# Two pairs of plain tiles instead of four in the second and third feed-forward blocks of a decoder trunk, with ten seven-product blocks instead of nine

## The chip, the cores and the metric

One NeuronCore of a Trainium2 chip. The metric is the device time of one execution of the whole kernel in microseconds, the median over the runs shown.

## The reference

Two layers run on x of 512 x 1024 in float32. Each layer is

```
h += 1/2 SwiGLU(RMSNorm(h));  h += Mixer(RMSNorm(h));  h += 1/2 SwiGLU(RMSNorm(h))
def swiglu(x, w_in, w_out):
    gate, up = jnp.split(x @ w_in, 2, axis=-1)      # w_in 1024 x 5632, w_out 2816 x 1024
    return (jax.nn.silu(gate) * up) @ w_out
```

The first layer's mixer is sparse attention with top-k keys, the second's a gated MLP over chunks of 128 positions; a last RMSNorm follows. So there are four feed-forward blocks: the first before the attention, the second and third directly one after the other, the fourth at the end.

## The kernel before, in words

**Data.** The stream `h` lies transposed in SBUF, as 8 tiles of 128 features by 512 positions. Each matrix product is done in three passes (`mul3`, L345): weights and activations are split into a high and a low part (fp32r), and high x high, high x low and low x high are added up in PSUM. XH[k], XL[k] are the two parts of the input times the norm's gain. The norm's own factor is multiplied in afterwards, at the gates and at the output.

**Weights.** `WeightStream` loads all weights in one order, PLAN (L47 to L51). A letter "P" is one load of 8 tiles of 128 x 128 and one unit; a letter "S" is one block of the seven-product form: four loads (r11, r21, r22, r12) and seven units F0 to F6. A unit is converted before use: ScalarE writes the high part (L184), VectorE the low part (L187). `_prepare` (L140) does the additions that some of the F units need, on VectorE: two sums at L158 for F1 and F2, L161 for F4, L163 for F5. They are issued one unit ahead, between the high and the low part of the unit before. The converted units lie in a ring `w` of three, and F units also in a ring `x` of two; at a unit "P" the converter goes up to four units ahead as far as the rings allow (`_next`, L196), and after each product of a form block up to five (`ahead`, L207).

**A feed-forward block** (`ffn`, L415) has 22 gate tiles and 22 up tiles of 128 features, in 22 pairs. Its input product runs plainly for the first four pairs and in the seven-product form for the other 18:

- A *group* (L355) computes two pairs in four PSUM banks, eight steps k of 12 matmuls with 512 columns (128 weights x 512 positions). Its weights are units P0 to P3, two k each. Hooks after the steps place the norm and the sums: after k = 3 the split of the squares (`parts_of_squares`), after k = 5 the column sums on TensorE (L384), VectorE's wait for them (`vcol`, L387) and the reciprocal root, after k = 7 the factor spread over rows (L394 on TensorE, then the copies `rb`, `rh` on ScalarE).
- `sums(kp)` (L448) builds for each pair of k tiles the four sums that the form needs, TH[kp] and TL[kp]: two scaled copies on ScalarE (L453), four differences on VectorE (L455 to L458), then two splits, each a copy `th` on ScalarE and a difference `tl` on VectorE (L370, L371). sums(0), (1), (2) are issued after k = 5, 6, 7 and sums(3) behind `plain_gates`, the multiplication of the gates by the norm (L497).
- `rest` (L590 to L616): four single products, for pairs 2 and 3, 24 matmuls of 512 columns each.
- Then blocks of the form. `two_pairs` (L508) computes two pairs in seven products of 24 matmuls with 256 columns, in three banks A, B, C. `right(f, kp)` says what a product reads: products 0, 3 and 5 read XH, XL, products 1, 2, 4 and 6 read TH, TL, for the four kp one after the other:

```
product(0, A, True, True, "m1")     # XH, XL; then ScalarE copies A
product(1, C, True, True, "m5")     # TH[kp][:, 0], TL[kp][:, 0], kp = 0..3
product(2, A, False, True, "u2")    # adds into A
```

The form blocks come in three chunks (2, 4 and 3 of them); after each chunk the output product adds its part to `h`. The first block has hooks of its own and another order; the fourth ends with the last norm.

**Order.** The order on each engine is that of the program (a manual schedule); VectorE, ScalarE and SyncE's queue of loads run theirs one after the other. `step` and `later` put the gates' further work (up, as_y) behind the products.

Of the kernel before, what the change touches and what calls it, by code (L numbers as in the profile page):

```python
# [19 lines left out]
P = 128  # L20
D = 1024
S = 512
KD = D // P
# [20 lines left out]
HALF = S // 2  # L44


PLAIN = 4  # L47
CHUNKS = (2, 4, 3)
FFN_PLAN = "P" * 8 + "SS" + "P" * 8 + "SSSS" + "P" * 8 + "SSS" + "P" * 6
PLAN = FFN_PLAN + "P" * 37 + FFN_PLAN + FFN_PLAN + "P" * 72 + FFN_PLAN  # L50
LAST = 2 * CHUNKS[-1]  # L51
WARM = 24
N_LOADS = sum(4 if k == "S" else 1 for k in PLAN)
N_PIECES = N_LOADS * LOAD
# [3 lines left out]
class WeightStream:  # L58
# [8 lines left out]
    def __init__(self, nc, pool, dram):  # L67
# [3 lines left out]
        self.loads, self.units = [], []  # L71
        for kind in PLAN:
            base, n = len(self.units), len(self.loads)
# [93 lines left out]
    def _convert_to(self, n):  # L167
        while self.converted < min(n, len(self.units)):
            u = self.converted
            kind, i, f = self.units[u]  # L170
            kept = u >= len(self.units) - LAST
            rings = [r for r in ("w", "x")[:1 if kind == "P" and not kept else 2]
                     if self._free(r, len(self.units) - LAST if kept else self.current)
                     and self._free(r, self.current)]
# [67 lines left out]
def tile_trunk(ctx: ExitStack, tc, specs_out, xT, wst, gT, gl, rel, onehot, bu, bv, lng, lnb, wspT, bsp, out):  # L242
# [10 lines left out]
    def uname(s):  # L253
        counter[0] += 1
        return f"{s}_{counter[0]}"
# [8 lines left out]
    def bank(tag="acc"):  # L264
        return psum.tile([P, 512], F32, tag=tag, bufs=4, name=uname(tag))
# [38 lines left out]
    acc = [None]  # L304
# [40 lines left out]
    def mul3(ps, w, x, first, last, **kw):  # L345

        (wh, wl), (xh, xl) = w, x
        mm(ps, wh, xh, start=first, stop=False, **kw)  # L348
        mm(ps, wh, xl, start=False, stop=False, **kw)  # L349
        mm(ps, wl, xh, start=False, stop=last, **kw)  # L350
# [14 lines left out]
    def single(ps, c, K, spec, parts=x_parts):  # L365
        for k in range(K):
            mul3(ps, W.take(spec(k, c)), parts(k), k == 0, k == K - 1)
# [5 lines left out]
    def parts_of_squares():  # L373

        ah = small.tile([P, S], F32R, tag="s0_512", bufs=1, name=uname("ah"))
        al = small.tile([P, S], F32R, tag="s1_512", bufs=1, name=uname("al"))
        split(acc[0], ah, al)
        return ah, al
# [33 lines left out]

        return {k: parts, k + 1: columns, k + 2: rows}

    def ffn(layer, which, norm, finish, begin=None, hooks=None, aside=None, last=None, tags=("acc", "aux")):  # L415

# [3 lines left out]

        NJ = DFF // P
        KP = KD // 2
        tag_of = lambda i: tags[i % 2]
        n1, n2 = slice(0, HALF), slice(HALF, S)
        with tc.tile_pool(name=uname("ffn"), bufs=1) as fp:
            W.spool = fp
# [4 lines left out]
            def gate_tile():  # L433
                return fp.tile([P, 2, S], F32, tag="gate", bufs=2, name=uname("gate"))
# [13 lines left out]
            def sums(kp):  # L448

                xg, t = [temp("m1"), temp("m5")], [temp("u2"), temp("u3")]  # L450
                for i in range(2):
                    k = 2 * kp + i
                    nc.scalar.activation(xg[i], H[k], AF.Copy, scale=g_sb[:, norm, k:k + 1])  # L453
                tt = nc.vector.tensor_tensor
                tt(t[0][:, n1], xg[0][:, n2], xg[0][:, n1], op=ALU.subtract)  # L455
                tt(t[0][:, n2], xg[1][:, n2], xg[0][:, n2], op=ALU.subtract)
                tt(t[1][:, n1], xg[1][:, n2], t[0][:, n1], op=ALU.subtract)
                tt(t[1][:, n2], xg[1][:, n1], t[1][:, n1], op=ALU.subtract)  # L458
                for i in range(2):
                    split(t[i], *(x[kp][:, 2 * i:2 * i + 2].rearrange("p a b -> p (a b)") for x in (TH, TL)))  # L460
# [15 lines left out]
            R, Y, later = {}, [], []  # L476
# [10 lines left out]
            def step():  # L487
                for _ in range(min(1, len(later))):
                    later.pop(0)()
# [5 lines left out]
            def plain_gates(banks, g):  # L495
                for i in range(2):
                    nc.vector.tensor_tensor(g[:, i], banks[2 * i], R["b"], op=ALU.mult)  # L497

            def plain_pairs(banks, g):
                nc.scalar.activation(g, g, AF.Silu)  # L500

                def up():
                    for i in range(2):
                        nc.vector.tensor_tensor(g[:, i], g[:, i], banks[2 * i + 1], op=ALU.mult)
                later.append(up)
                later.append(lambda: as_y(g))
# [59 lines left out]
            def scale():  # L566
                R["ps"] = R.get("ps") or bank(tags[1])
                R["c"] = scale_columns(R["ps"], R["sq"])

            def spread():  # L570
                R["b"], R["h"] = scale_rows(R["c"], R["ps"])
# [13 lines left out]

            banks = [bank(tags[0]) for _ in range(4)]
            group(banks, [0, NJ, 1, NJ + 1], KD, spec_in, hooks={k: lambda k=k: hook(k) for k in range(KD)})
            g = [gate_tile() for _ in range(2)]
            R["ps"] = R.get("ps") or bank(tags[1])
            rest = [bank(tags[1]) for _ in range(2)]  # L590
            if not hooks:
                plain_gates(banks, g[0])
            single(rest[0], 2, KD, spec_in)
            if hooks:
                R["sq"] = parts_of_squares()
                scale()
            else:
                plain_pairs(banks, g[0])
                sums(3)
            single(rest[1], NJ + 2, KD, spec_in)  # L600
            if hooks:
                spread()
                plain_gates(banks, g[0])
            step()
            rest.append(bank(tags[1]))
            single(rest[2], 3, KD, spec_in)
            step()
            if hooks:
                plain_pairs(banks, g[0])
            plain_gates(rest, g[1])  # L610
            rest.append(bank(tags[1]))
            single(rest[3], NJ + 3, KD, spec_in)
            step()
            if hooks:
                step()
            plain_pairs(rest, g[1])  # L616
            done, n_dp = 0, 0
            for ci, dps in enumerate(CHUNKS):
                p0 = done
                if ci:  # L620
                    Y.clear()
                done += 2 * dps
                if ci == 0:
                    done += PLAIN
                for i in range(dps):
                    pair = PLAIN + 2 * n_dp
                    between = ()
                    if aside:
                        aside(n_dp)
                    if last and n_dp == sum(CHUNKS) - 1:  # L630
                        between = last[0](bank("acc"), gate_tile)
                    two_pairs(pair, tag_of(n_dp), between)
                    n_dp += 1
                flush()
                n_k = done - p0
                tag0 = tag_of(n_dp)
                tag1 = tag_of(n_dp + 1)

                def spec_out(k, c, p0=p0):
                    return ("ffn_w_out", (layer, which), (p0 + k) * P, [(0, c * P, P)])  # L640

                def y_parts(k, s=slice(0, S)):
                    return Y[k // 2][0][:, k % 2, s], Y[k // 2][1][:, k % 2, s]

                end = ci == len(CHUNKS) - 1
                if end and last:
                    W.extra = [x[0].rearrange("p a b -> p (a b)") for x in (TH, TL)]
                    last[1](n_k, spec_out, y_parts, R["c"], temp)
                    continue
                if end:  # L650
                    W.spool = None

                def add(j, ps):
                    t = gate_tile()[:, 0]
                    nc.vector.tensor_tensor(t, ps, R["h"], op=ALU.mult)
                    nc.vector.tensor_tensor(H[j], H[j], t, op=ALU.add)
                    if end:
                        finish(j)

                first = [bank(tag0) for _ in range(4)]  # L660
                group(first, range(4), n_k, spec_out, y_parts)
                for j in range(4):
                    add(j, first[j])
                for j in range(4, KD):
                    ps = bank(tag1)
                    single(ps, j, n_k, spec_out, y_parts)
                    add(j, ps)
# [415 lines left out]
    def into(norm):  # L1083
        return lambda j: prepare(j, norm)
# [10 lines left out]
    with tc.tile_pool(name="bias", bufs=1) as bp:  # L1095
        table, dist = [], []

        def begin(spare):
# [4 lines left out]
        ffn(0, 0, 0, into(1), begin, {k: lambda k=k: behind(k) for k in range(KD)},  # L1103
            aside=lambda i: 0 < i <= HEADS and spread_bias(*dist, i - 1))
    mixer_a(dist[1], 2)
    ffn(0, 1, 2, into(3))
    ffn(1, 0, 3, into(4), tags=("aux", "acc"))
    mixer_b(5)


# [137 lines left out]
```

## Time and profile before

| | |
|---|---|
| median of 3 runs | 2093.56 us (2093.43 to 2094.03) |
| the profiled execution | 2093.53 us, of it a span of 2091.7 us |
| granted TensorE clock, mean | 0.998 of full speed |
| VectorE, ScalarE, GpSimd busy | 71%, 43%, 4% of the span |
| matmuls | 12252 |
| read from HBM | 205.67 MB, 101 GB/s over the span |
| second, third feed-forward block: first matmul | 621.8, 968.3 us |

The times of the rows further down count from the start of the span. Each operation has a line of the program; where a helper issues it, the name of what it writes tells the place. TensorE's matmuls are pipelined, so the distance between two starts, not the duration of one, is what one costs.

### The profile page before, as it was taken

What the parts mean: (1) busy time and instruction counts of PE and PEld (TensorE: products, weight loads), DVE (VectorE), ACT (ScalarE), POOL (GpSimd) and SP (SyncE); (2) the same over time, 40 slices, a digit from 0 to 9 for tenths busy, and PEclk for the clock granted to TensorE, in tenths of its full rate; (3) what the DMA queues carried; (4) which work ended last, traced back from release to release, by engine and by line L of the source; (5) the groups of instructions that cost most, each with busy time, mean ns of one, the idle gap of its engine ahead of it and who ended that gap; (6) DMA issues with size and microseconds to landing.
All of it is one profiled execution on the core that took longest, in us unless ns stands there. A gap on an engine that the chain in (4) does not pass through costs nothing.

```text
span 2091.7 us, 29771 instructions
## 1 busy us (share of the span) xinstructions
PE 2076.6 (99%) x12252; PEld 1844.4 (88%) x12252; DVE 1476.7 (71%) x2046; ACT 894.3 (43%) x1157; POOL 78.1 (4%) x57
## 2 busy tenths in 40 slices
PE   8999999999999999999999999999999999999998
PEld 7989898888888999898989999888888888989897
DVE  7768686597767678677968677645846466778676
ACT  6535344434446345354625344432323245535253
POOL 0000000143200000000000000000000000000000
PEclk9999999999999999999999999999999999999999
DMA  4233332222123222222333222422222222323321
GB/s 174 98 117 109 112 110 92 100 96 90 68 72 110 101 101 101 101 101 82 111 106 107 101 102 81 152 91 91 91 101 83 89 91 91 111 94 109 110 93 71
DMA packets 59001, 209.72 MB, mean 100 GB/s; under 512 B 6824, under 2 KB 6872, under 8 KB 58736
## 3 DMA queue, kind: packets, MB, share of 16 engines
q1 hardware_dynamic: 55584, 198.73, 27.4%
q0 software_dynamic: 1408, 5.38, 0.8%
q10 hardware_dynamic: 1872, 3.70, 0.5%
q8 instruction: 96, 1.57, 0.3%
q14 instruction: 41, 0.34, 0.1%
HBM read 205.67 MB, written 4.74 MB: 101 GB/s over the span
## 4 chain that ended last, share of the span: by engine, by line
PE 97%; DVE 2%; ACT 1%; issue 0%; ACTq 0%; DVEq 0%
PE acc L348 16%; PE acc L349 16%; PE acc L350 16%; PE aux L348 12%; PE aux L350 12%; PE aux L349 12%; PE acc L990 1%; PE aux L992 1%; PE aux L990 1%; PE acc L992 1%; PE acc L991 1%; PE aux L991 1%; PE aux L1040 1%; PE acc L908 1%; PE aux L872 1%; PE aux L896 0%
## 5 line engine op out<-in xcount | busy, mean ns | idle before, releaser
L187 DVE TENSOR_TENSOR wlo<-raw,whi 128x1024 fp32r<-128x1024 f32 (+1 forms) x382 | 463.4, 1218 | 296.7 <-ACT whi L184 296.3
L184 ACT ACTIVATE whi<-raw 128x1024 fp32r<-128x1024 f32 (+1 forms) x409 | 426.2, 1050 | 470.4 <-PE acc L349 192.0
L348 PE MATMUL acc<-xh,whi 128*128 128x512 f32 (+1 forms) x864 | 299.2, 346 | 1.7 <-ACT xh L309 1.6
L349 PE MATMUL acc<-xl,whi 128*128 128x512 f32 (+1 forms) x864 | 289.5, 335 | 1.1 <-DVE xl L310 1.1
L350 PE MATMUL acc<-xh,wlo 128*128 128x512 f32 (+1 forms) x864 | 289.1, 335 | 0.0
L348 PE MATMUL aux<-xh,whi 128*128 128x256 f32 (+1 forms) x616 | 196.9, 320 | 0.0
L350 PE MATMUL aux<-xh,wlo 128*128 128x256 f32 (+1 forms) x616 | 196.5, 319 | 0.0
L349 PE MATMUL aux<-xl,whi 128*128 128x256 f32 (+1 forms) x616 | 196.4, 319 | 0.0
L348 PEld LDWEIGHTS acc<-xh,whi 128*128 128x128 f32 x864 | 164.8, 191 | 20.0 <-ACT xh L309 2.6
L349 PEld LDWEIGHTS acc<-xl,whi 128*128 128x128 f32 x864 | 165.0, 191 | 18.7 <-DVE xl L310 2.0
L350 PEld LDWEIGHTS acc<-xh,wlo 128*128 128x128 f32 x864 | 164.8, 191 | 16.9
L348 PE MATMUL acc<-th,whi 128*128 128x256 f32 x608 | 172.4, 284 | 0.0
L350 PE MATMUL acc<-th,wlo 128*128 128x256 f32 x608 | 172.1, 283 | 0.0
L349 PE MATMUL acc<-tl,whi 128*128 128x256 f32 x608 | 172.0, 283 | 0.0
L348 PE MATMUL aux<-th,whi 128*128 128x256 f32 x544 | 154.0, 283 | 0.0
L349 PE MATMUL aux<-tl,whi 128*128 128x256 f32 x544 | 154.0, 283 | 0.0
L350 PE MATMUL aux<-th,wlo 128*128 128x256 f32 x544 | 154.0, 283 | 0.0
L348 PE MATMUL acc<-yh,whi 128*128 128x512 f32 x328 | 127.7, 389 | 0.0
L349 PE MATMUL acc<-yl,whi 128*128 128x512 f32 x328 | 127.7, 389 | 0.0
L348 PE MATMUL aux<-yh,whi 128*128 128x512 f32 x328 | 127.6, 389 | 0.0
L349 PE MATMUL aux<-yl,whi 128*128 128x512 f32 x328 | 127.6, 389 | 0.0
L350 PE MATMUL acc<-yh,wlo 128*128 128x512 f32 x328 | 127.6, 389 | 0.0
(292 smaller groups left out, 4404.9 us busy)
## 6 DMA issues: line engine op xcount, KB each, us to landing
raw<-in_wst SPq DMA_DIRECT2D x372, 512.0 KB, 3.2
dist<-dist_rows ACTq DMA_DIRECT2D x8, 320.0 KB, 4.2
h<-in_xT SPq DMA_DIRECT2D x8, 256.0 KB, 6.4
tb<-dist POOLq DMA_DIRECT2D x8, 256.0 KB, 3.9
bias<-in_bv POOLq DMA_DIRECT2D x1, 1536.0 KB, 7.5
raw<-in_wst SPq DMA_DIRECT2D x2, 256.0 KB, 3.5
wT<-in_wspT POOLq DMA_DIRECT2D x1, 512.0 KB, 9.3
bs<-in_bsp POOLq DMA_DIRECT2D x1, 512.0 KB, 11.4
```

The source lines that it names most:

```text
L184: self.nc.scalar.activation(hi[:, s], src[:, s], AF.Copy)
L187: self.lo_engine.tensor_tensor(lo[:, s], src[:, s], hi[:, s].bitcast(F32), op=ALU.subtract)
L348: mm(ps, wh, xh, start=first, stop=False, **kw)
L349: mm(ps, wh, xl, start=False, stop=False, **kw)
L350: mm(ps, wl, xh, start=False, stop=last, **kw)
L872: mm(ps[:, :n], QK[h, 0][:, b * P:(b + 1) * P], QK[h, 1][:, :n], start=True, stop=True)
L908: mm(po[0][:, b * P:(b + 1) * P], V[j][:, h * P:(h + 1) * P], pT[:, j * P:(j + 1) * P], start=j == 0, stop=j == b)
L990: mm(banks[t], xh, wh, start=k == 0, stop=False)
L991: mm(banks[t], xl, wh, start=False, stop=False)
L992: mm(banks[t], xh, wl, start=False, stop=k == KD - 1)
L1040: mm(ps[:, t * P:(t + 1) * P], V[t][:, d * P:(d + 1) * P], wT[:, g, :], start=True, stop=True)
```

## The change

The second and third feed-forward blocks are called with `plain=2`: only the group's two pairs run plainly, `rest` is left out, and 20 pairs run in the form, in chunks of 3, 4 and 3 blocks. `plain_gates`, `sums(3)` and `plain_pairs` then follow the group directly, and the first form block stands behind them. PLAN has, for these two blocks, four "P" fewer at the head and one "S" more. `tag_of` is shifted by one there, so that the first form block takes the banks that `rest` had. The other two blocks keep `plain=4` with the same order as before.

```diff
-PLAIN = 4
-CHUNKS = (2, 4, 3)
-FFN_PLAN = "P" * 8 + "SS" + "P" * 8 + "SSSS" + "P" * 8 + "SSS" + "P" * 6
-PLAN = FFN_PLAN + "P" * 37 + FFN_PLAN + FFN_PLAN + "P" * 72 + FFN_PLAN
+BLOCKS = {4: (2, 4, 3), 2: (3, 4, 3)}
+def ffn_plan(plain):
+    chunks = BLOCKS[plain]
+    return "P" * 2 * plain + "".join("S" * n + "P" * (2 * n + plain * (i == 0)) for i, n in enumerate(chunks))
+PLAN = ffn_plan(4) + "P" * 37 + ffn_plan(2) + ffn_plan(2) + "P" * 72 + ffn_plan(4)
...
-        tag_of = lambda i: tags[i % 2]
+        chunks = BLOCKS[plain]
+        tag_of = lambda i: tags[(i + (plain == 2)) % 2]
...
             group(banks, [0, NJ, 1, NJ + 1], KD, spec_in, hooks={k: lambda k=k: hook(k) for k in range(KD)})
-            g = [gate_tile() for _ in range(2)]
+            g = [gate_tile() for _ in range(plain // 2)]
             R["ps"] = R.get("ps") or bank(tags[1])
...
+            if plain == 2:
+                plain_gates(banks, g[0])
+                sums(3)
+                plain_pairs(banks, g[0])
+            else:
+                rest = [bank(tags[1]) for _ in range(2)]
...
-                    pair = PLAIN + 2 * n_dp
+                    pair = plain + 2 * n_dp
...
-    ffn(0, 1, 2, into(3))
-    ffn(1, 0, 3, into(4), tags=("aux", "acc"))
+    ffn(0, 1, 2, into(3), plain=2)
+    ffn(1, 0, 3, into(4), plain=2, tags=("aux", "acc"))
```

## Rows read from the trace of the kernel before

**Rows 1.** The profile's page: the busy time of each engine (part 1, with its share of the span and its instructions in brackets), and the weight loads of part 6 (count, KB each, median us from issue to landing).

```profile
PE 2076.6 (99%) x12252; PEld 1844.4 (88%) x12252; DVE 1476.7 (71%) x2046; ACT 894.3 (43%) x1157; POOL 78.1 (4%) x57
...
raw<-in_wst SPq DMA_DIRECT2D x372, 512.0 KB, 3.2
```

**Rows 2.** The waits of TensorE over the whole span: which instruction waited for which, us in total, times, longest us. The two rows that lie in the first feed-forward block.

```profile
PE acc L348 <- ACT xh L309: 1.6, 1, 1.6
PE acc L349 <- DVE xl L310: 1.1, 2, 0.8
```

**Rows 3.** Stretches of the third feed-forward block: from and to (us from the span's start), length, then busy us and instructions of TensorE, its weight loads, VectorE, ScalarE and GpSimd, the granted TensorE clock, the DMA share and GB/s. First the four single products of `rest`, then the first and the second block of the seven-product form.

```profile
991.83:1013.71 21.88, 21.88 (x99) 18.12 (x98) 19.35 (x30) 14.64 (x20) 0.00 (x0) 1.00 0.27 97
1013.71:1033.87 20.16, 20.16 (x170) 20.15 (x169) 19.75 (x22) 12.35 (x15) 0.00 (x0) 1.00 0.30 105
1033.87:1054.03 20.16, 20.16 (x171) 20.16 (x170) 14.36 (x16) 9.36 (x11) 0.00 (x0) 1.00 0.31 105
```

**Rows 4.** VectorE in order of time in the third feed-forward block, from the end of the norm's preparation to the first form block: start us, us, engine, line, operation, output and inputs, count, and in brackets the idle time before it and what ended it.

```profile
977.00 2.36 DVE L187 TENSOR_TENSOR wlo<-raw,whi 128x1024 fp32r<-128x1024 f32 x2
979.27 0.69 DVE L371 TENSOR_TENSOR al<-sqacc,ah 128x512 fp32r<-128x512 f32 x1
...
985.64 0.16 DVE L387 TENSOR_SCALAR vcol<-acc 128x4 f32<-128x4 f32 x1 [4.13 <-PE acc L384]
...
991.10 1.23 DVE L187 TENSOR_TENSOR wlo<-raw,whi 128x1024 fp32r<-128x1024 f32 x1 [0.26 <-ACT whi L184]
992.24 0.42 DVE L455 TENSOR_TENSOR u<-m 128x256 f32<-128x256 f32 x1
...
993.71 1.48 DVE L371 TENSOR_TENSOR tl<-u,th 128x512 fp32r<-128x512 f32 x2
996.08 0.42 DVE L455 TENSOR_TENSOR u<-m 128x256 f32<-128x256 f32 x1 [0.89 <-ACT m L453]
...
999.22 1.28 DVE L497 TENSOR_TENSOR gate<-aux,rb 128x512 f32<-128x512 f32 x2
1000.42 1.22 DVE L187 TENSOR_TENSOR wlo<-raw,whi 128x1024 fp32r<-128x1024 f32 x1
1002.25 0.43 DVE L455 TENSOR_TENSOR u<-m 128x256 f32<-128x256 f32 x1 [0.61 <-ACT m L453]
...
1006.88 1.22 DVE L158 TENSOR_TENSOR wsum<-raw,raw 128x1024 f32<-128x1024 f32 x1
...
1011.42 1.28 DVE L504 TENSOR_TENSOR gate<-gate,aux 128x512 f32<-128x512 f32 x2
...
1014.94 1.22 DVE L161 TENSOR_TENSOR raw<-raw,raw 128x1024 f32<-128x1024 f32 x1
```

**Rows 5.** ScalarE in the same stretch, same columns.

```profile
993.03 0.64 ACT L370 ACTIVATE th<-u 128x512 fp32r<-128x512 f32 x1 [0.74 <-DVE u L456]
993.83 0.63 ACT L370 ACTIVATE th<-u 128x512 fp32r<-128x512 f32 x1 [0.16 <-DVE u L458]
...
995.32 1.34 ACT L453 ACTIVATE m<-h,g_sb 128x512 f32<-128x512 f32 x2
...
997.95 0.63 ACT L370 ACTIVATE th<-u 128x512 fp32r<-128x512 f32 x1 [0.16 <-DVE u L458]
...
1000.54 1.06 ACT L500 ACTIVATE gate<-gate 128x1024 f32<-128x1024 f32 x1 [1.01 <-DVE gate L497]
...
1016.85 0.60 ACT L528 ACTIVATE m<-aux 128x512 f32<-128x512 f32 x1 [0.72 <-PE aux L350]
```

**Rows 6.** TensorE in the same stretch, same columns: the first product of the norm's columns, its rows, and the first matmul of `rest`.

```profile
984.66 0.17 PE L384 MATMUL acc<-ones_r,ah 128*128 128x2 f32 x1
...
991.03 1.05 PE L394 MATMUL acc<-ident,nwy 128*128 128x128 f32 x8
991.83 0.48 PE L348 MATMUL acc<-xh,whi 128*128 128x512 f32 x1
```

**Rows 7.** All engines in order of time in the second feed-forward block, same columns: the norm's rows on TensorE, plain_gates on VectorE, and the table load ahead of Silu on ScalarE.

```profile
644.45 1.05 PE L394 MATMUL aux<-ident,nwy 128*128 128x128 f32 x8
...
652.63 1.28 DVE L497 TENSOR_TENSOR gate<-acc,rb 128x512 f32<-128x512 f32 x2
...
652.96 1.28 ACT L500 ACT_TABLE_LOAD   x1
```

**Rows 8.** Two stretches of the first feed-forward block, columns as in rows 3.

```profile
32.00:36.00 4.00, 3.09 (x8) 2.28 (x9) 3.97 (x8) 2.97 (x7) 0.00 (x0) 0.75 0.58 201
36.00:40.00 4.00, 4.00 (x16) 3.16 (x15) 3.66 (x9) 3.35 (x7) 0.00 (x0) 0.82 0.16 64
```

**Rows 9.** TensorE in order of time at the start of the kernel and in the first feed-forward block, columns as in rows 4.

```profile
2.91 5.38 PE L289 MATMUL aux<-ones_r 128*128 128x128 f32 x24 [2.91 <-ACT ones_r L286]
...
9.48 0.63 PE L348 MATMUL acc<-xh,whi 128*128 128x512 f32 x1
...
10.46 0.40 PE L348 MATMUL acc<-xh,whi 128*128 128x512 f32 x1
...
32.10 0.50 PE L348 MATMUL acc<-xh,whi 128*128 128x512 f32 x1 [1.60 <-ACT xh L309]
...
33.98 0.59 PE L348 MATMUL acc<-xh,whi 128*128 128x512 f32 x1
...
37.35 0.43 PE L350 MATMUL acc<-xh,wlo 128*128 128x512 f32 x1
```

More of the change, by code (lines that the diff above doesn't have):

```diff
@@ L44 @@
 HALF = S // 2
-PLAIN = 4
-CHUNKS = (2, 4, 3)
-FFN_PLAN = "P" * 8 + "SS" + "P" * 8 + "SSSS" + "P" * 8 + "SSS" + "P" * 6
-PLAN = FFN_PLAN + "P" * 37 + FFN_PLAN + FFN_PLAN + "P" * 72 + FFN_PLAN
-LAST = 2 * CHUNKS[-1]
+BLOCKS = {4: (2, 4, 3), 2: (3, 4, 3)}
[3 more added lines that the diff above has]
+PLAN = ffn_plan(4) + "P" * 37 + ffn_plan(2) + ffn_plan(2) + "P" * 72 + ffn_plan(4)
+LAST = 2 * BLOCKS[4][-1]
 WARM = 24
@@ L413, in norm_hooks, with ffn @@
         return {k: parts, k + 1: columns, k + 2: rows}
-    def ffn(layer, which, norm, finish, begin=None, hooks=None, aside=None, last=None, tags=("acc", "aux")):
+    def ffn(layer, which, norm, finish, begin=None, hooks=None, aside=None, last=None, plain=4, tags=("acc", "aux")):
         NJ = DFF // P
         KP = KD // 2
-        tag_of = lambda i: tags[i % 2]
+        chunks = BLOCKS[plain]
+        tag_of = lambda i: tags[(i + (plain == 2)) % 2]
         n1, n2 = slice(0, HALF), slice(HALF, S)
@@ L587, in ffn @@
             group(banks, [0, NJ, 1, NJ + 1], KD, spec_in, hooks={k: lambda k=k: hook(k) for k in range(KD)})
-            g = [gate_tile() for _ in range(2)]
+            g = [gate_tile() for _ in range(plain // 2)]
             R["ps"] = R.get("ps") or bank(tags[1])
-            rest = [bank(tags[1]) for _ in range(2)]
-            if not hooks:
+            if plain == 2:
                 plain_gates(banks, g[0])
[L593 to L596, printed above, removed]
-            else:
-                plain_pairs(banks, g[0])
-                sums(3)
@@ L600, in ffn @@
[L600 to L614, printed above, removed]
-                step()
@@ L616, in ffn @@
-            plain_pairs(rest, g[1])
+                sums(3)
+                plain_pairs(banks, g[0])
+            else:
+                rest = [bank(tags[1]) for _ in range(2)]
+                if not hooks:
+                    plain_gates(banks, g[0])
+                single(rest[0], 2, KD, spec_in)
+                if hooks:
+                    R["sq"] = parts_of_squares()
+                    scale()
+                else:
+                    plain_pairs(banks, g[0])
+                    sums(3)
+                single(rest[1], NJ + 2, KD, spec_in)
+                if hooks:
+                    spread()
+                    plain_gates(banks, g[0])
+                step()
+                rest.append(bank(tags[1]))
+                single(rest[2], 3, KD, spec_in)
+                step()
+                if hooks:
+                    plain_pairs(banks, g[0])
+                plain_gates(rest, g[1])
+                rest.append(bank(tags[1]))
+                single(rest[3], NJ + 3, KD, spec_in)
+                step()
+                if hooks:
+                    step()
+                plain_pairs(rest, g[1])
@@ L617, in ffn @@
             done, n_dp = 0, 0
-            for ci, dps in enumerate(CHUNKS):
+            for ci, dps in enumerate(chunks):
                 p0 = done
@@ L623, in ffn @@
                 if ci == 0:
-                    done += PLAIN
+                    done += plain
                 for i in range(dps):
-                    pair = PLAIN + 2 * n_dp
+                    pair = plain + 2 * n_dp
                     between = ()
@@ L629, in ffn @@
                         aside(n_dp)
-                    if last and n_dp == sum(CHUNKS) - 1:
+                    if last and n_dp == sum(chunks) - 1:
                         between = last[0](bank("acc"), gate_tile)
@@ L643, in y_parts @@
                     return Y[k // 2][0][:, k % 2, s], Y[k // 2][1][:, k % 2, s]
-                end = ci == len(CHUNKS) - 1
+                end = ci == len(chunks) - 1
                 if end and last:
```

## The prediction

> **What bounds the kernel.** I first read the busy shares: TensorE is busy for 2076.6 of 2091.7 us, VectorE for 71% [rows 1]. Then TensorE's waits: all that it ever waits for outside the very start is 2.7 us in the first feed-forward block, for XH and XL [rows 2]. So time is saved only by fewer or shorter matmuls, and anything late for TensorE adds in full. Last I read the stretches around the change [rows 3]: in the third block the four products that the change removes (`rest`, L597 to L617) take 21.88 us, and a block of the seven-product form takes 20.16 us. But VectorE is busy for 19.35 us in the first and 19.75 us in the second. The removed stretch is not spare for it: it is where the sums TH, TL of the form are finished. That is where I look for the cost.
>
> **1. Matmuls.** Per block 4 x 8 x 3 = 96 matmuls of 512 columns go, 7 x 2 x 4 x 3 = 168 of 256 columns come. By rows 3 that is -21.88 + 20.16 = -1.72 us, and -3.44 us for both blocks. The columns fall by an eighth (49152 to 43008), the time by less: 21.88/96 is 228 ns a matmul, 20.16/168 is 120 ns, so about 2 x 120 - 228 = 12 ns of each does not depend on its columns, and there are 72 more of them. The Trainium skill (TensorE: Matmul & The Clock Gate, Back-to-back issue gap) puts the fixed part of a warm matmul at about 2.5 ns, which would save 96 x 215.8 - 168 x 109.2 ns = 2.4 us a block; the trace does not agree, and the measured stretches decide. The sum at the end would be 1.3 us lower by that rule.
>
> **2. What is issued earlier.** Loads are as many as before: four for the form block as for the four units "P" that it replaces, so the loads cost nothing as long as TensorE's pace covers them. The converted units change. Units P0 to P3 feed the group of four banks. Where before P4 to P6 were converted, it is now F0 and F1 at P1, F2 at P2, F3 at P3, with the VectorE operations of the form (L158 twice, L161) among them. Rows 4 show their like before the old first form block: L158, lo, L158, lo are four operations in 1011.42 - 1006.88 = 4.54 us. In the third block they stand ahead of `al`: from 979.27 they end at 983.81, `al` (0.69) at 984.50. The column products that read it start at 984.66 [rows 6]. So this costs 0, covered by the 4.13 us that VectorE idled before `vcol` [rows 4], with 0.2 us to spare; if the load for L158 landed a whole load late it would be 3.2 us [rows 1]. F2's lo ends about 985.6, with `vcol` at 985.64: 0 again. F3 takes the place of the unit at 991.10; ahead of it L161 for F4 is new: 1.14 us less the 0.26 us that VectorE idled there, +0.87 us for all that is behind it on VectorE.
>
> **3. The sums come too late.** The first form block now begins where `rest` began, at 991.83 [rows 6]. Its product 0 reads XH, XL and lasts 24 x 0.12 = 2.88 us. Product 1 reads TH, TL of all four pairs, one after the other, 0.36 us each, so pair 3 is wanted at 991.83 + 2.88 + 1.08 = 995.8. Before, sums(3) only began at 1002.25 [rows 4], under `rest`. What it needs now, in VectorE's order (it is in program order, behind `vcol`):
> - sums(1) at 992.24 + 0.87 = 993.1 [rows 4]; sums(2), old 996.08, is at 996.95. Its ACT inputs (995.32) come behind the two sums before and rb, rh, and move with it [rows 5].
> - plain_gates, old 999.22 to 1000.42, now 1000.1 to 1001.3.
> - sums(3) then starts at once: the L187 of old 1000.42 is gone, and ACT has its inputs ready by about 1000.7, since it is past sums(2) at 997.95 + 0.63 + 0.87 and the two inputs take 1.3.
> - From the first L455 to th is 993.03 - 992.24 = 0.79, to tl 993.71 - 992.24 = 1.47 plus 0.69 [rows 4, 5]: th starts at 1002.1, the first tl is there at 1003.5.
> TensorE's second matmul of pair 3 (L349) would have run at 995.9, and runs at 1003.5: a stall of 7.6 us, with a scrap of work for pair 2 in the middle of it. Bounds: 6.7 without L161 in the way; 10.8 with a late load. In the second block the rows stand the same distance apart: gates come 8.18 us after the row products (652.63, 644.45), in the third 8.19 [rows 4, 6, 7]. So 7.6 us in both.
>
> **4. The clock after it.** In the first block TensorE waited 1.60 us once and then had little work; the nine matmuls of 512 columns that start from 33.98 to 37.35 are 0.42 apart, and the granted clock of the two stretches is 0.75 and 0.82 [rows 8, 9]. That is the 1.2 GHz level for a part of them, and the eight gaps lost 3.37 - 8 x 0.228 = 1.55 us. Here the wait is longer, so I take that row: 1.55 us a block. Low end 0. High end twice it, 3.1: at the kernel's start TensorE worked from 2.91, and its matmuls still lasted 0.63 at 9.48, and 0.40 only at 10.46 [rows 9].
>
> **5. Behind the stall.** Product 2 adds into bank A, which ACT must first have copied (`m1`). ACT is behind the second th of sums(3) (993.83 - 992.24 later than L455, ends 1003.5), then Silu (1.06) and the copy (0.60) [rows 5]: done by 1005.1. TensorE with half the clock ends product 1 at about 1003.5 + 14 x 0.21 = 1006.4 (0.21 is my estimate, half of the 0.42 of point 4 for half the columns), so nothing is added. In the second block a table load of 1.28 us stands ahead of Silu [rows 7]: 1006.4, just covered; with the full clock product 1 would end at 1005.2 and this wait would cost 1.2 us. In the rest of the first form block VectorE had 0.4 us to spare before [rows 3]; now one plain pair (gates, up, yl) and four conversions fewer stand behind it and the stall gives it time, so I take 0, and 3 us a block as the high end: the yh conversion, the copies u2 and two lo's queued one behind the other on ACT and VectorE. Three form blocks in a row in the first chunk cost nothing: the second in the old kernel leaves VectorE at 14.36 of 20.16 [rows 3], and four in a row stood in the second chunk before. Banks: R["ps"] and A, B, C are the four of one tag, nothing is reused; four y pairs in the first chunk as before.
>
> **Sum.** Per block -1.72 + 7.6 + 1.55 = +7.43, twice: +14.9. The profiled execution took 2093.53 us (span 2091.7), within 0.03 of the median 2093.56, so 2093.5 + 14.9 = **2108.4 us**, 0.7% slower.
>
> **Rivals.**
> - *The clock holds through the stall.* For it: pair 2 gives TensorE a little work in between. Against: rows 8, 9, after a shorter wait. Then 7.6 - 1.72 in the third block, 7.6 + 1.2 - 1.72 in the second: +13.0, 2106.5 us.
> - *A second wait in the first form blocks* (ACT's queue of copies, yh and conversions, point 5; or `al` late, point 2). For it: VectorE's 98% in the old first form block, and 0.2 us of margin at `al`. Against: 9 us of stall in which both catch up. 2.5 to 3 us a block more: 2113.5 to 2114.5 us.
> - *The other side: the sums are in time,* and only the -3.44 is left: 2090.1 us, 0.16% under before. The place is the last tl of pair 3 against product 1. It decides at 995.9 (third block): VectorE would have to reach sums(3) 7.6 us earlier than I work out. For it: VectorE idles 4.13 us before `vcol`, and sums(0) to sums(3) don't need the norm at all, only its place in the queue. Against: the code issues sums(0) behind `scale()`, and the old rows show each sum behind `vcol` in just that order. By the Trainium skill's fixed part (TensorE: Matmul & The Clock Gate, Back-to-back issue gap; point 1) this case would be 2088.8, 0.23% faster.
>
> **Chances.** 0.65 for the forecast, 0.15 for the clock that holds, 0.10 for the second wait, 0.10 for sums in time. A measurement of this kernel tells about 0.2% (4.2 us) from no change. The first three are slower by more; the last is within 0.2%, but for a little that I leave for a larger saving: faster 0.02, same 0.08, slower 0.90. The range goes from a stall of 6.7 us with the clock held and the table load hidden (2 x (6.7 - 1.72) = +10, 2103.5) to the second wait's upper end, 2114.5. It leaves the case of sums in time outside.
>
> **What would show it.** In the changed profile: TensorE's waits name L349 aux/acc <- tl and DVE L371 in the second and third block, two or three waits in each of about 7 us together, in product 1 and nowhere else; granted clock under 1 in the 4 us after; 144 matmuls more (12396); L161 ahead of sums(1); no wait at the column products; the later form blocks at 20.16 us. I am wrong if product 1 runs through, or if the stall is there but stands at a copy of A, at weights (wlo), or at the column products; and if the form blocks after it are longer than 20.2 us, the price was in VectorE's load and not in the sums' place.

## The result and the profile after

| | before | after |
|---|---|---|
| median | 2093.79 us (2093.43 to 2094.03, 4 runs) | 2109.94 us (2108.69 to 2110.78, 4 runs) |
| ratio | | 1.0076 (95% interval 1.0064 to 1.0089) |
| profiled execution: time, span | 2093.53, 2091.7 us | 2110.78, 2109.1 us |
| granted TensorE clock | 0.998 | 0.993 |

The change makes the kernel 16.2 us slower. The page of the changed kernel has the 144 matmuls more, and a span that is longer by 17.4 us (the profiled execution is the longest of the four):

```profile
span 2109.1 us, 30100 instructions
...
PE 2082.3 (99%) x12396; PEld 1855.6 (88%) x12396; DVE 1495.3 (71%) x2064; ACT 904.0 (43%) x1171; POOL 78.1 (4%) x57
```

TensorE's waits over the whole span of the changed kernel that the kernel before does not have (which instruction waited for which, us in total, times, longest us). All of these are in the second and third feed-forward block, at the matmuls that read TH and TL (L348 and L349 of before are L354 and L355 here):

```profile
PE acc L354 <- ACT th L376: 5.4, 2, 2.9
PE aux L354 <- ACT th L376: 5.4, 2, 2.9
...
PE aux L355 <- DVE tl L377: 0.5, 2, 0.3
PE acc L355 <- DVE tl L377: 0.5, 2, 0.4
```

VectorE in the third block of the changed kernel, answering to [rows 4]; a line number is 6 or 7 higher than there (L158, L161, L187, L371, L387 are L164, L167, L193, L377, L393; L455 is L462, L497 is L504). Columns: start us, us, engine, line, operation, output and inputs, idle time before:

```profile
992.89 0.69 DVE L377 TENSOR_TENSOR al<-sqacc,ah 128x512 fp32r<-128x512 f32 x1
...
994.72 0.16 DVE L393 TENSOR_SCALAR vcol<-acc 128x4 f32<-128x4 f32 x1
...
999.84 1.22 DVE L167 TENSOR_TENSOR raw<-raw,raw 128x1024 f32<-128x1024 f32 x1
...
1002.11 0.42 DVE L462 TENSOR_TENSOR u<-m 128x256 f32<-128x256 f32 x1
...
1009.08 1.28 DVE L504 TENSOR_TENSOR gate<-aux,rb 128x512 f32<-128x512 f32 x2
1010.27 0.41 DVE L462 TENSOR_TENSOR u<-m 128x256 f32<-128x256 f32 x1
...
1011.73 1.47 DVE L377 TENSOR_TENSOR tl<-u,th 128x512 fp32r<-128x512 f32 x2
```

`al` now stands behind the conversions and starts at 992.89, with `vcol` at 994.72 and no idle time before it where VectorE had 4.13 us. L167 (999.84) stands ahead of sums(1) (1002.11) as the prediction had it, the gates follow sums(2) at once, sums(3) begins at 1010.27, and its first tl (1011.73) is the one that TensorE waits for. The same stretch on TensorE, answering to [rows 6]: the norm's columns at 993.73, its rows at 1000.10, and product 0 of the form from 1000.91:

```profile
993.73 0.17 PE L390 MATMUL acc<-ones_r,ah 128*128 128x2 f32 x1
...
1000.10 1.05 PE L400 MATMUL acc<-ident,nwy 128*128 128x128 f32 x8
1000.91 0.36 PE L354 MATMUL acc<-xh,whi 128*128 128x256 f32 x1
...
1007.69 0.38 PE L354 MATMUL acc<-th,whi 128*128 128x256 f32 x1 [2.87 <-ACT th L376]
1008.43 0.58 PE L355 MATMUL acc<-tl,whi 128*128 128x256 f32 x1 [0.35 <-DVE tl L377]
...
1011.74 0.58 PE L354 MATMUL acc<-th,whi 128*128 128x256 f32 x1 [2.52 <-ACT th L376]
1012.47 0.58 PE L355 MATMUL acc<-tl,whi 128*128 128x256 f32 x1 [0.15 <-DVE tl L377]
...
1018.18 0.37 PE L354 MATMUL acc<-th,whi 128*128 128x256 f32 x1
```

Pair 2 is waited for at 1007.69 and pair 3 at 1011.74, each time first for th, then for tl. Had nothing been late, the second matmul of pair 3 would have run at 1000.91 + 2.88 + 1.08 + 0.12 = 1004.99; it ran at 1012.47, 7.48 us late. From there to the second form block, which starts at 1031.23, are 18.76 us; at the pace of [rows 3] they would be 20.16 - 4.08 = 16.08. The other 2.68 us are the clock. Stretches of the same block (columns as in [rows 3]):

```profile
1008.00:1012.00 4.00, 1.13 (x4) 0.76 (x3) 3.87 (x9) 2.44 (x5) 0.00 (x0) 0.52 0.00 0
1012.00:1016.00 4.00, 3.85 (x17) 3.55 (x18) 3.35 (x4) 3.88 (x6) 0.00 (x0) 0.50 0.00 0
1016.00:1020.00 4.00, 4.00 (x27) 4.00 (x26) 4.00 (x6) 2.62 (x4) 0.00 (x0) 0.70 0.55 195
1020.00:1024.00 4.00, 4.00 (x35) 4.00 (x35) 3.23 (x4) 2.51 (x3) 0.00 (x0) 1.00 0.18 72
```

The granted clock is 0.52 and 0.50 (the 1.2 GHz level) from 1008 to 1016, and whole again only after 1018. The second form block then takes 20.16 us (1031.23 to 1051.39), as before, without a wait. The second feed-forward block loses the same: its first form block goes from 645.92 to 676.23, 30.31 us, the third's from 1000.91 to 1031.23, 30.32 us. So a block costs 30.32 - 21.88 = 8.44 us more than `rest` did, both 16.9 us. The rest of the span's 17.4 us lies before the second block, which begins 0.67 us later (622.43 and 621.76), in code that has not changed: in the eight kernels here that have the first feed-forward block of before, the second begins between 621.65 and 622.43.

### The profile page after: what moved, and what is told of

Read it like the earlier page. It is cut to its first block, busy times and chain, and to the rows that moved or that the text cites. A ratio compares the mean times of both kernels' runs of the same rounds, so it can differ in the third digit from the quotient of the medians.

```text
span 2109.1 us, 30100 instructions
## 1 busy us (share of the span) xinstructions
PE 2082.3 (99%) x12396; PEld 1855.6 (88%) x12396; DVE 1495.3 (71%) x2064; ACT 904.0 (43%) x1171; POOL 78.1 (4%) x57
## 4 chain that ended last, share of the span: by engine, by line
PE 93%; DVE 4%; ACT 1%; issue 1%; ACTq 0%; DVEq 0%
PE acc L355 15%; PE acc L354 15%; PE acc L356 15%; PE aux L355 12%; PE aux L354 12%; PE aux L356 11%; PE acc L1002 1%; PE aux L1003 1%; PE acc L1003 1%; PE aux L1002 1%; PE aux L1004 1%; PE acc L1004 1%; PE aux L1052 1%; PE acc L920 1%; PE aux L884 1%
## 5 line engine op out<-in xcount | busy, mean ns | idle before, releaser
L193 DVE TENSOR_TENSOR wlo<-raw,whi 128x1024 fp32r<-128x1024 f32 (+1 forms) x384 | 465.6, 1217 | 302.2 <-ACT whi L190 302.0
L354 PE MATMUL acc<-xh,whi 128*128 128x256 f32 (+1 forms) x856 | 293.6, 343 | 1.7 <-ACT xh L315 1.6
L355 PE MATMUL acc<-xl,whi 128*128 128x256 f32 (+1 forms) x856 | 283.9, 332 | 1.1 <-DVE xl L316 1.1
L356 PE MATMUL acc<-xh,wlo 128*128 128x256 f32 (+1 forms) x856 | 283.7, 331 | 0.0
L354 PE MATMUL aux<-xh,whi 128*128 128x256 f32 (+1 forms) x608 | 191.5, 315 | 0.0
L355 PE MATMUL aux<-xl,whi 128*128 128x256 f32 (+1 forms) x608 | 191.0, 314 | 0.0
L354 PE MATMUL acc<-th,whi 128*128 128x256 f32 x640 | 182.9, 286 | 5.4 <-ACT th L376 5.4
L355 PE MATMUL acc<-tl,whi 128*128 128x256 f32 x640 | 182.8, 286 | 0.5 <-DVE tl L377 0.5
L356 PE MATMUL acc<-th,wlo 128*128 128x256 f32 x640 | 182.4, 285 | 0.0
L354 PEld LDWEIGHTS acc<-xh,whi 128*128 128x128 f32 x856 | 163.4, 191 | 18.8 <-ACT xh L315 2.6
L355 PEld LDWEIGHTS acc<-xl,whi 128*128 128x128 f32 x856 | 163.6, 191 | 17.5 <-DVE xl L316 2.0
L354 PE MATMUL aux<-th,whi 128*128 128x256 f32 x576 | 164.5, 286 | 5.4 <-ACT th L376 5.4
L355 PE MATMUL aux<-tl,whi 128*128 128x256 f32 x576 | 164.7, 286 | 0.5 <-DVE tl L377 0.5
L356 PE MATMUL aux<-th,wlo 128*128 128x256 f32 x576 | 164.3, 285 | 0.0
L354 PEld LDWEIGHTS acc<-th,whi 128*128 128x128 f32 x640 | 124.2, 194 | 5.9 <-ACT th L376 5.9
L354 PE MATMUL acc<-yh,whi 128*128 128x512 f32 x328 | 127.7, 389 | 0.0
L355 PE MATMUL acc<-yl,whi 128*128 128x512 f32 x328 | 127.7, 389 | 0.0
L354 PE MATMUL aux<-yh,whi 128*128 128x512 f32 x328 | 127.6, 389 | 0.0
L355 PE MATMUL aux<-yl,whi 128*128 128x512 f32 x328 | 127.6, 389 | 0.0
```

The costliest lines, as they stand in the source:

```text
L193: self.lo_engine.tensor_tensor(lo[:, s], src[:, s], hi[:, s].bitcast(F32), op=ALU.subtract)
```

## The experiments

Nine kernels, each timed beside the kernel before on the same chip. The times of the kernel before were 2093.2 to 2094.6 us in all of them. Most of them weigh two theories: mine, that sums and copies stand too late in VectorE's and ScalarE's queues; and the rival, that the form block itself, or VectorE's load, costs more than the plain pairs.

### One block alone

```diff
-    ffn(1, 0, 3, into(4), plain=2, tags=("aux", "acc"))
+    ffn(1, 0, 3, into(4), tags=("aux", "acc"))       # and ffn_plan(4) for the third block in PLAN
```

> Only the second feed-forward block is changed (two plain pairs, ten form blocks); the third keeps four pairs and nine. My theory, that each changed block pays by itself for sums that come too late (from the two traces 10.2 us of wait and slow clock, less 1.72 us of saved matmuls, so +8.4 us a block): about 2093.8 + 8.4 = 2102.2 us, with the waits of product 1 in the second block alone. Rival, that the two blocks harm one another (the second passes a backlog on to the third) or that only one of them pays: 2094 or 2110 us.

Measured: 2101.3 us (2100.87 to 2101.65), ratio 1.0036 (1.0023 to 1.0049), 7.5 us more than before. TensorE's waits at TH and TL, two of each, are left in the second block alone:

```profile
PE aux L354 <- ACT th L376: 5.7, 2, 2.9
...
PE aux L355 <- DVE tl L377: 0.5, 2, 0.3
```

Half the change costs about half (7.5 of 16.2): each block pays by itself.

### No wait for the sums

```diff
             def right(f, kp):
+                if R.get("plain_x"):                                  # set for the first form block of a changed ffn
+                    return XH[2 * kp][:, n1], XL[2 * kp][:, n1]
```

> The first form block of the second and third feed-forward block reads XH, XL in every product in place of the sums TH, TL; the sums are still computed, and the later form blocks read them. So the wait for the sums is gone and all other work stays. If the late sums are the only thing that holds product 1, TensorE runs through and the saved matmuls are left: 2093.8 - 3.4 = 2090.4 us. My theory adds a second lock at nearly the same place: the copy of A after product 0 stands on ScalarE behind sums(3) and Silu, and product 2 writes into A, so it can't begin before that copy (1013.9 in the trace of the changed kernel, 7.2 us after product 2 could have begun). Then the wait moves from product 1 to product 2 and is about as long (7.2 us and the slow clock, some 9.5 a block): 2093.8 + 2 x (9.5 - 1.72) = 2109.4 us, TensorE waiting for ACT's copy m.

This kernel leaves TH and TL out of the products of its first form blocks; it is run for its time alone. Measured: 2110.44 us (2110.00 to 2111.35), ratio 1.0079 (1.0062 to 1.0096): nothing is gained. The waits have moved, as expected, from th and tl to the copy of bank A on ScalarE:

```profile
PE aux L354 <- ACT m L537: 8.5, 1, 8.5
PE acc L354 <- ACT m L537: 7.0, 1, 7.0
```

So there are two locks at nearly the same place. TensorE would have waited as long for the first copy of A, which stands behind sums(3) and Silu on ScalarE. In the second block it is longer, 8.5 us against 7.0; the table load of 1.28 us ahead of Silu [rows 7] is most of the difference.

### TensorE kept busy through the wait

```diff
                     for p in range(2):
                         for kp in range(KP):
                             s = slice((p * KP + kp) * P, (p * KP + kp + 1) * P)
+                            if fill and f == 1 and p == 0 and kp > 1:      # first form block, product 1, pairs 2 and 3
+                                for _ in range((26, 24)[kp - 2]):
+                                    mm(B[:, :HALF], wh[:, s], XH[0][:, n1], start=True, stop=True, skip_group_check=True)
```

> As the changed kernel, with 26 matmuls of 256 columns that nobody reads ahead of pair 2 and 24 ahead of pair 3 in product 1 of the first form block (into bank B, which product 3 starts anew), 3.1 and 2.9 us, to fill the two waits. If the slow clock after the waits is 2.7 us of the loss in each block, as the two traces say, it stays at full speed and 2 x 2.7 = 5 us come back: about 2110 - 5 = 2105 us, granted clock 0.998 again. If the clock costs nothing beside the waits: 2110 us or a little more, for the matmuls that are too many.

Measured: 2107.11 us (2106.89 to 2107.70), ratio 1.0064 (1.0049 to 1.0079), 2.8 us less than the change and not 5. The clock stays whole in the third block:

```profile
1008.00:1012.00 4.00, 3.65 (x29) 3.29 (x28) 3.87 (x9) 2.44 (x5) 0.00 (x0) 1.00 0.00 0
1012.00:1016.00 4.00, 4.00 (x36) 4.00 (x35) 3.45 (x4) 3.62 (x5) 0.00 (x0) 1.00 0.10 26
```

Most of the rest is taken back by the second lock, in the second block:

```profile
PE aux L354 <- ACT m L538: 1.0, 1, 1.0
...
PE aux L354 <- ACT u L538: 0.2, 1, 0.2
```

In the third block the first form block shrinks from 30.32 to 27.96 us (999.30 to 1027.26): that is the clock, 2.36 us. In the second it shrinks by 0.9 us only: TensorE at full speed reaches product 2 before the copy of A is done and waits 0.98 us for it, then 0.16 us for u2. This is the wait that the prediction's rival gave 1.2 us for a clock that holds.

### Sums ahead of the gates

```diff
             if plain == 2:
-                plain_gates(banks, g[0])
                 sums(3)
-                plain_pairs(banks, g[0])                 # now behind product 0 and its copy of A
+                plain_gates(banks, g[0])
```

> In the changed blocks sums(3) stands ahead of plain_gates, and Silu of the plain pair behind the first copy of A; the work is the same. If the place in VectorE's and ScalarE's queues sets the wait: the first tl of pair 3 comes about 1 us earlier (1.19 us of gates less 0.25 us in which the scaled copies are not there yet), so 2110 - 2 x 0.95 = 2108 us, less if the clock recovers sooner. If it is the load of VectorE as such, whatever its order: 2110 us, no change.

Measured: 2107.39 us (2107.15 to 2108.43), ratio 1.0066 (1.0051 to 1.0081): 2.5 us less than the change, with the same work. TensorE in the third block:

```profile
998.08 1.05 PE L400 MATMUL acc<-ident,nwy 128*128 128x128 f32 x8
...
1008.81 0.58 PE L354 MATMUL acc<-th,whi 128*128 128x256 f32 x1 [1.91 <-ACT th L376]
1009.55 0.58 PE L355 MATMUL acc<-tl,whi 128*128 128x256 f32 x1 [0.15 <-DVE tl L377]
```

The rows product is at 998.08, so the second matmul of pair 3 runs 11.47 us after it and not 12.37 as in the changed kernel: 0.9 us a block is the order. From it to the second form block (1027.63) are 18.08 us, in the changed kernel 18.76: the other 0.7 us is the clock. In the second block TensorE then waits 0.5 us at product 4 for the copy u2, which it does not in the changed kernel; 2 x 1.6 - 0.5 = 2.7 us, near the 2.5 measured.

### Sums much earlier, with GpSimd's help

```diff
+                if plain == 2:                            # in hook(k), behind step k of the group
+                    if k == 0:
+                        R["sq"] = parts_of_squares(); W.lo_engine = nc.gpsimd
+                    elif k == 5:
+                        scale()
+                    elif k == 7:
+                        spread(); W.lo_engine = nc.vector
+                    if k in (1, 2, 5, 6):
+                        sums((1, 2, 5, 6).index(k))
+                    return
...
-            tt(r21, r11, r21, op=ALU.subtract)
+            self.lo_engine.tensor_tensor(r21, r11, r21, op=ALU.subtract)      # gates and Silu behind the copy of A
```

> The changed kernel with another order in the second and third feed-forward blocks, nothing left out: the split of the squares behind k = 0, sums(0) and sums(1) behind k = 1 and 2, ahead of VectorE's wait for the column products, sums(2) and sums(3) behind k = 5 and 6; the gates and Silu of the plain pair behind the first copy of A; and the low parts of P3 and F0 to F3 with F4's difference on GpSimd, which is idle there. My theory: the loss is the place of the sums in the queues, so the first tl of pair 3 comes about 8 us earlier, just when product 1 wants it, the copy of A is no longer behind Silu, the clock stays up, and only the saved matmuls are left: 2093.8 - 3.4 = 2090.4 us, up to 2092 with a wait of 0.5 us here and there. Rival, that ten form blocks cost VectorE more than it can give whatever the order: waits of several us stay, in product 1 or later, 2096 us or more.

Measured: 2115.91 us (2115.36 to 2116.91), ratio 1.0104 (1.0086 to 1.0122). This expectation was wrong by 25 us. First the longest of TensorE's waits, then VectorE and GpSimd in the third block:

```profile
PE acc L400 <- DVE nwy L307: 8.8, 1, 8.8
PE aux L400 <- DVE nwy L307: 3.4, 1, 3.4
```

```profile
991.43 3.31 DVE L164 TENSOR_TENSOR wsum<-wsum,raw 128x1024 f32<-128x1024 f32 x1
994.66 2.61 DVE L462 TENSOR_TENSOR u<-m 128x256 f32<-128x256 f32 x1
...
1001.90 0.16 DVE L393 TENSOR_SCALAR vcol<-acc 128x4 f32<-128x4 f32 x1
...
1002.29 2.36 DVE L303 TENSOR_SCALAR nwy<-nwi 128x4 int32<-128x4 int32 x1
```

```profile
990.61 6.38 POOL L193 TENSOR_TENSOR wlo<-raw,whi 128x1024 fp32r<-128x1024 f32 x2 [337.16 <-ACT whi L190]
996.95 2.57 POOL L193 TENSOR_TENSOR wlo<-wsum,whi 128x1024 fp32r<-128x1024 f32 x1
```

While GpSimd works on its low parts, a difference of 256 columns takes VectorE 2.61 us where it else takes 0.42, and L164 3.31 where it takes 1.22 [rows 4]. VectorE so reaches `vcol` at 1001.90. Behind it two instructions of the norm on 128 x 4 elements take 2.36 and 2.26 us (1002.29 and 1004.69) in place of 0.17 and 0.16, beside GpSimd's next two (2.34 us each, from 1002.28 and 1004.58). So the norm's rows (L400) come 8.8 us late. The Trainium skill (SBUF — State Buffer, SBUF: two separate sides) says that the two engines share one pair of ports, that whichever starts first holds it for a whole instruction while the other is blocked, and that VectorE needs it, among other cases, where it reads two SBUF operands. The trace agrees: VectorE's 2.61 us from 994.66 end at 997.27, 0.3 us after GpSimd's two (990.61 + 6.38 = 996.99). My addition had taken GpSimd for free.

### The same without GpSimd

```diff
-                        R["sq"] = parts_of_squares(); W.lo_engine = nc.gpsimd
+                        R["sq"] = parts_of_squares()              # all low parts and F4's difference stay on VectorE
```

> As early, but all low parts and F4's difference stay on VectorE. By my durations VectorE then reaches its wait for the column products some 4 us late in the third block (vcol's chain ends about 2.7 us after the rows want it), and the first tl of pair 3 another 2.4 us late; in the second block, where VectorE has less to do before, 1 to 2 us in all. So 2093.8 - 3.4 + 6.5 = about 2097 us, to 2100 with the slow clock: order alone gives most of the loss back, the rest is VectorE's work ahead of the form blocks. If order alone is the cause: 2090.4 us as early. If it is the load alone: 2108 to 2110 us.

Measured: 2104.47 us (2102.95 to 2104.81), ratio 1.0046 (1.0031 to 1.0061), 11.4 us under the kernel with GpSimd and 5.5 us under the change. TensorE's waits:

```profile
PE acc L400 <- DVE nwy L307: 3.2, 1, 3.2
...
PE acc L354 <- ACT u L535: 2.4, 1, 2.4
PE aux L354 <- ACT u L535: 2.4, 1, 2.4
...
PE acc L355 <- DVE tl L377: 0.4, 1, 0.4
```

One more, 1.0 us for `al`, lies in the first feed-forward block. Neither changed block waits for th any more, and only the third for 0.4 us of tl. What is left has other names: the rows product of the third block, 3.2 us, by VectorE's work ahead of `vcol` (expected 2.7); and, not expected, 2.4 us in each block at product 4, for the copy u2. ScalarE stands there behind Silu, which waits for the gates, which I had put behind two conversions. So order gives back a part, and the two engines' queues are so full there that what is moved ahead makes something else late.

### Sums and copies in time, in the second block, and in both

```diff
+                    at = (1, 5, 6, 7) if layer else (1, 2, 5, 6)         # third and second block: steps k of sums(0) to (3)
+                    if k in at:
+                        sums(at.index(k))                                # squares at k = 0, scale at 5, spread at 7
...
-                    for p in range(2):
-                        for kp in range(KP):
+                    for kp in range(KP):
+                        for p in range(2):
...
             if plain == 2:
                 plain_gates(banks, g[0])
-                sums(3)
-                plain_pairs(banks, g[0])                                 # now behind product 2 and its copy u2
```

In the kernel for both blocks F3 of the third block's first form block is converted only after the group.

> Only the second feed-forward block is changed, and its sums are moved ahead without GpSimd: the squares behind k = 0, sums(0) and (1) behind k = 1 and 2, sums(2) and (3) behind k = 5 and 6; the gates stay ahead of the first form block, Silu stands behind the copy u2, and each product of every form block takes the four kp in the outer loop, so pair 3 is wanted 1.1 us later. In the run before (early_one_engine) this block's sums were there in time and only the copy u2, behind Silu and the late gates, cost 2.4 us. My theory, that the loss of the changed kernel is nothing but the place of the sums and of that copy: no wait in the second block, the clock stays up and the saved matmuls are left, 2094.0 - 1.7 = 2092.3 us. Rival, that a form block in place of the plain pairs costs something by itself (contention, VectorE's backlog): 2094 us or more.

Measured: 2092.16 us (2091.76 to 2092.58, 11 runs) beside 2093.81 us (2093.21 to 2094.55, 21 runs) of the kernel before, ratio 0.9992 (0.9983 to 1.0001): 1.65 us less, where the saved matmuls were worth 1.72. The slowest of its runs is under the fastest of before, though the interval of the ratio touches 1. Sums, Silu and the order of kp are moved at once here, and this run does not part them. In the trace TensorE has no wait in the second block. From the block's first matmul to that of the third it takes 345.08 us (622.09 to 967.17), before 346.58 (621.76 to 968.34): 1.50 us less, as its first form block lasts 20.41 us and not 20.16. The profiled executions as a whole are 1.46 us apart (2092.07 and 2093.53), though the newer one waits 1.0 us more in the first feed-forward block, for `al`. Two stretches of the first form block (columns as in [rows 3]):

```profile
648.00:652.00 4.00, 4.00 (x34) 3.88 (x34) 3.87 (x9) 3.29 (x6) 0.00 (x0) 1.00 0.64 246
652.00:656.00 4.00, 4.00 (x35) 4.00 (x35) 3.79 (x4) 3.31 (x6) 0.00 (x0) 1.00 0.21 65
```

> As in_time_second, with the third block changed too. There VectorE comes out of the norm's preparation some 5 us later in the block than in the second, so sums(1) to (3) stand behind the column products (k = 5, 6, 7) and F3 is converted only after the group. By durations of the earlier traces the first tl of pair 3 is 1 to 2 us late: 2 us of wait for 1.7 us of saved matmuls, so about what in_time_second takes, 2092 to 2094 us. If VectorE's load is no matter and only the order is: 2090.6 us. If the third block's wait is 4 us or more, the durations that I add up leave something out: 2096 us.

Measured: 2096.57 us (2096.10 to 2096.88, 11 runs), ratio 1.0013 (1.0004 to 1.0022). The third block loses: 4.4 us more than the second alone. TensorE there, then stretches of it:

```profile
990.99 0.36 PE L355 MATMUL acc<-xh,whi 128*128 128x256 f32 x1
...
998.66 0.58 PE L355 MATMUL acc<-th,whi 128*128 128x256 f32 x1 [2.40 <-ACT th L377]
```

```profile
996.00:1000.00 4.00, 1.44 (x7) 0.94 (x6) 2.80 (x7) 3.34 (x7) 0.00 (x0) 0.78 0.00 0
1000.00:1004.00 4.00, 4.00 (x20) 4.00 (x20) 3.97 (x6) 1.89 (x2) 0.00 (x0) 0.50 0.12 26
1004.00:1008.00 4.00, 4.00 (x32) 4.00 (x31) 3.80 (x4) 3.11 (x5) 0.00 (x0) 0.87 0.87 305
```

The wait is 2.4 us for th and 0.15 for tl, a little over the 1 to 2 us that I had added up. The first form block takes 25.97 us (990.99 to 1016.96); 25.97 - 20.16 - 2.55 = 3.26 us are the clock, which I had left out, or up to 0.25 us less, since in the second block the same form block takes 20.41 us without a wait. So 2.55 + 3.26 - 1.72 = +4.1 us, near the 4.4 measured.

### The fourth block too

```diff
-PLAN = ffn_plan(4) + "P" * 37 + ffn_plan(2) + ffn_plan(2) + "P" * 72 + ffn_plan(4)
+PLAN = ffn_plan(4) + "P" * 37 + ffn_plan(2) + ffn_plan(4) + "P" * 72 + ffn_plan(2)
...
-    ffn(1, 1, 5, None, last=(last_block, last_product))
+    ffn(1, 1, 5, None, last=(last_block, last_product), plain=2)        # order as in the second block
```

> in_time_second with the fourth feed-forward block changed in the same way (two plain pairs, ten form blocks, sums behind k = 1, 2, 5, 6), the third and first as before. In the trace of the kernel before VectorE ends the norm's preparation 3.5 us after the fourth block's first matmul, as in the second (3.3 us) and not as in the third (9 us). If that free time is what decides, the fourth block gives its 1.7 us too: 2092.2 - 1.7 = 2090.4 us, no wait of TensorE in product 1. If the second block was a lucky place, or the last block's own work (turning back, the final norm) needs VectorE: 2092 us or more.

Measured: 2090.70 us (2090.30 to 2091.23, 11 runs) beside 2094.01 us (15 runs), ratio 0.9984 (0.9975 to 0.9993). It is the fastest of all kernels here, 3.3 us under the kernel before and 19.2 under the change; its interval leaves out 1. TensorE's waits in it are, beside the start, those that the kernel before has as well ([rows 2], and 0.3 us in the attention, which the prediction's 2.7 us left out):

```profile
PE acc L355 <- ACT xh L316: 1.6, 1, 1.6
PE acc L356 <- DVE xl L317: 1.1, 2, 0.8
PE acc L935 <- ACT pT L925: 0.3, 1, 0.3
```

What the fourth block shares with the second is read from the kernel before: VectorE's last instruction on the input, in the second and in the third block.

```profile
624.49 0.69 DVE L339 TENSOR_TENSOR sqacc<-sqacc,sq 128x512 f32<-128x512 f32 x1
...
976.39 0.68 DVE L339 TENSOR_TENSOR sqacc<-sqacc,sq 128x512 f32<-128x512 f32 x1
```

It ends 3.4 us after the block's first matmul (621.76) in the second block, 8.7 us after it (968.34) in the third, and in the fourth again 3.4 us (1735.86 and 1732.45).

## Why the prediction was right

**Direction and mechanism.** Forecast 2108.4 us (2103.5 to 2114.5), measured 2109.9. The waits stand where they were put: product 1 of the first form block, pairs 2 and 3, for th and tl, in both blocks, with product 0 and the column products untouched. One sign was named wrongly: the waits were to stand at tl, two or three of about 7 us together, and there are four, of 5.9 us in each block, 5.4 of them at th, which comes first. The lateness of point 3 is counted between the starts of matmuls and is longer than the waits.

**1. Matmuls: right.** -1.72 us a block by the two stretches; the second block with its sums in time gave 1.65 us (1.50 between its marks in the trace), second and fourth together 3.3 us for 3.44. An estimate with the Trainium skill's fixed part of 2.5 ns for a warm matmul (TensorE: Matmul & The Clock Gate, Back-to-back issue gap) makes that 2.4 and 4.8 us; the runs agree with the rows.

**2. What is issued earlier: right.** `al` was put at 984.50, 0.16 ahead of the column products. On the later clock of the new trace it starts 0.84 us before them (992.89 and 993.73) and lasts 0.69, so it ends 0.15 ahead: no wait. L167 stands where it was put.

**3. The sums: right.** 7.6 us forecast, 7.48 measured, and not by luck: on the old clock (9.08 us less) sums(1), the gates and sums(3) start at 993.03, 1000.00 and 1001.19, forecast 993.1, 1000.1 and 1001.3. The one lock that was priced only behind the stall, the copy of A behind Silu, is hidden by it and shows when the sums are not waited for (7.0 and 8.5 us).

**4. The clock: the mis-sized term.** Forecast 1.55 us a block from one row of the first feed-forward block, upper end 3.1; measured 2.68 us in the profiled execution, 2.36 by keeping TensorE busy. In [rows 9] the nine slow matmuls after the wait took 3.4 us; here TensorE was slow from 1012.47 to 1018.18, 5.7 us, of which half, 2.85, is lost, near the 2.68 found. The forecast was 1.5 us low; this term alone, twice 0.8 to 1.1, makes up for that and a little more, and the stall, 0.1 us a block shorter than forecast, goes the other way. The spread of the change's runs (2108.7 to 2110.8) goes with the granted clock: 0.995 in the two shorter runs, 0.993 in the two longer.

**5. Behind the stall: right.** The next form block takes 20.16 us and nothing waits.

**Rivals.** "The clock holds" is refuted by the 0.50 of the stretches; made to hold, it takes 2107.1 us, for which that rival had 2106.5. "A second wait" was not there. "Sums in time" did not happen, but it was the true alternative: its 2090.1 us for two blocks is about what the second and the fourth block reached (2090.7) once the sums were in time.

## What to carry to other kernels

The matmuls that a change takes off TensorE may have been the cover for another engine's work: before a stretch is shortened, list what the other engines finish under it, and when the next stretch first reads each result. The shorter form paid in the two blocks where VectorE comes free 3.4 us into the block, and in no order tried here where it comes free 8.7 us in; that no order would do there is not shown. A wait of TensorE is to be priced with the clock behind it, which here cost another third to more than the whole of it.

## What the runs showed of the hardware

- GpSimd's two-operand instructions and VectorE's did not run side by side: 256 columns on VectorE took 2.61 us in place of 0.42, an instruction on 4 columns with one operand 2.36 in place of 0.17, and GpSimd's own 128 x 1024 went from 2.4 to 3.2 us (6.38 for two).
- After a wait of only 2.4 us the granted clock was 0.50 for a whole stretch of 4 us and cost 3.0 to 3.26 us, more than the wait. After 6 us of waits in two parts it cost 2.7 us.
